# The second MLP projection, product by product over the whole inner layer

## The chip, the cores and the metric

The kernel runs on one core of a Trainium2 chip. The metric is the device time of one execution in microseconds (us); lower is better. TensorE does the matmuls, VectorE, ScalarE and GpSimd the elementwise work, and SyncE only issues DMAs, one after the other, between HBM and the on-chip memory.

## The reference

One layer: a token mixer (pooling and gated DeltaNet) with its two projections, then a squared-ReLU MLP, then a last RMSNorm. The change concerns the MLP and the last norm. S = 1024 tokens, D_MODEL = 1024, D_FF = 4096, float32.

```
def reference(x, norm_mix, w_in, ..., norm_mlp, w_up, w_down, norm_final):
    h = x
    ...                                   # token mixer
    h = h + mix @ w_out[l]
    u = rms_norm(h, norm_mlp[l])
    h = h + jnp.square(jax.nn.relu(u @ w_up[l])) @ w_down[l]
    return rms_norm(h, norm_final)
```

## The kernel before, in words

Precision: each float32 operand is split into a rounded half ("hi", a cast on ScalarE) and the rest ("lo", a subtraction on VectorE). A product is three matmuls, hi x hi, hi x lo and lo x hi (`mm3`, line 44 in the profile). In names, `wh`/`wl` are hi and lo of a weight tile, `th`/`tl` and `sh`/`sl` those of other operands.

Both MLP projections use Strassen's scheme in Winograd's form: matrices are cut into 2 x 2 quadrants, and 7 products of quadrants, with sums of quadrants as operands, take the place of 8. Products are numbered 1 to 7.

First projection (`up_ready`, `up_product`): the 4096 columns of the inner layer are taken in 16 pairs of 2 x 128. Per pair, a weight tile `wu` (1 MB) is loaded, GpSimd makes four sums of weight blocks, and each product is split and multiplied, 12 matmuls of 128x128 by 128x512. The tokens' operands TH[i], TL[i] of all seven products are made once, at `turn_second`, in the stretch called "the turn" below; products 1 and 2 of pairs 0 and 1 run ahead of it. Results are combined in `p1`, `u2`, `u3` (VectorE adds a bank; product 1 is copied by ScalarE) and become four quadrants of the hidden matrix after relu and square on ScalarE (`hidden`, lines 953 and 954): h11, h21 (in p1's tile), h12 (in u2's), h22 (in u3's). Each is written to HBM, into `hd[b]`, where b counts blocks of four pairs.

Second projection (`block_load`, `down_ready`, `sums`, `down_product`): for each of 4 blocks, eight 1 MB tiles are loaded, a11 to a22 of the hidden matrix and b11 to b22 of the weights. A step (b, i, s) is one product i on half s of the block: a split of its two operands (two casts and two subtractions of 128x1024), and 24 matmuls, six into each of four banks. Between steps, GpSimd (line 1053) turns the loaded tiles in place into the sums that later products need. After a product's second half, VectorE adds its four banks to the residual `ht` (line 1093). In the last block, products 3, 7 and 4 are followed by `final`: the last norm of a token tile, out of place in a tile `o`, with products of `o` and the norm's weight partly on GpSimd.

```
TARGET = {1: (0, 0), 6: (0, 1), 7: (1, 1), 4: (1, 0), 2: (0, 0), 5: (1, 1), 3: (0, 1)}
todo = [(b, i, s) for b in range(NB) for i in (1, 2, 5, 6, 3, 7, 4) for s in range(2)]
```

The order on each engine: TensorE's is the order of the code; the other engines' instructions are placed by a scheduler, which the diff does not show. Tiles come from pools with a number of buffers (`bufs`); a new tile in a full pool waits until the oldest one's readers are done. A tile of a pool that was opened in the room of a closed one waits for the readers of what lay there.

Of the kernel before, what the change touches and what calls it, by code (L numbers as in the profile page):

```python
# [28 lines left out]
def hybrid_trunk(ctx, tc, x, norm_mix, w_in, conv_w, w_pool, pool_scale, a_log, dt_bias,  # L29
# [203 lines left out]
    u_r = const.tile([P, P], F32R, name="u_r")  # L233
# [16 lines left out]
    for l in range(7):  # L250
        b = 1 << l
        m = const.tile([P, P], F16, name=f"lev{l}")
# [142 lines left out]
    def pool_group(i, acc, g, dst):  # L395
# [17 lines left out]
        if i == 0:  # L413
            hd = const.tile([P, 16], F32, name="hd", tag="gr")
# [479 lines left out]
    NPAIR, BQ = FF // 256, 4  # L894
    NB = NPAIR // BQ

    hd = [hdp.tile([P, 4, BQ, HALF], F32, name=f"hd{b}") for b in range(NB)]
    H11, H12, H21, H22 = range(4)
    wuv = w_up2.rearrange("(k p) f -> p k f", p=P)

    def turn_second(ys):

        for k in range(KT):
# [3 lines left out]
            A.activation(R[12 if k < 4 else 22][:, j, :], pt, AF.Copy, scale=nmlp[:, k:k + 1])  # L907
            if k < 4:
                V.tensor_tensor(R[11][:, j, :], R[12][:, j, :], R[11][:, j, :], op=ALU.subtract)
            else:  # L910
                V.tensor_tensor(R[2][:, j, :], R[22][:, j, :], R[11][:, j, :], op=ALU.subtract)
                G.tensor_tensor(R[12][:, j, :], R[22][:, j, :], R[12][:, j, :], op=ALU.subtract)
                G.tensor_tensor(R[21][:, j, :], R[21][:, j, :], R[2][:, j, :], op=ALU.subtract)
        for i, r in ((6, 2), (7, 12), (5, 11), (4, 21), (3, 22)):
# [3 lines left out]
            for j in range(4):  # L918
                A.copy(TH[i][:, j, :], R[r][:, j, :])  # L919
                V.tensor_tensor(TL[i][:, j, :], R[r][:, j, :], TH[i][:, j, :].bitcast(F32), op=ALU.subtract)  # L920
# [31 lines left out]
    def hidden(p, c, src, dst):  # L952
        A.activation(dst, src, AF.Relu)
        A.activation(dst, dst, AF.Square)
        nc.sync.dma_start(out=hd[p // BQ][:, c, p % BQ, :], in_=dst)

    def up_product(p, i, w):
# [7 lines left out]
        if i == 1:  # L965
            m["p1"] = cp.tile([P, HALF], F32, name="p1", tag="c")
            A.copy(m["p1"], acc)
        elif i == 2:
            hidden(p, H11, acc, cp.tile([P, HALF], F32, name="h11", tag="c"))
# [3 lines left out]
        elif i == 7:  # L973
            m["u3"] = ws.tile([P, HALF], F32, name="u3", tag="raw", bufs=3)
            V.tensor_tensor(m["u3"], acc, m["p1"], op=ALU.add)
        elif i == 5:
            V.tensor_tensor(m["u3"], acc, m["u3"], op=ALU.add)
            hidden(p, H22, m["u3"], m["u3"])
        elif i == 4:
            V.tensor_tensor(m["p1"], acc, m["p1"], op=ALU.add)  # L980
            hidden(p, H21, m["p1"], m["p1"])
# [180 lines left out]
```

## Time and profile before

| | us |
|---|---|
| median of 3 runs | 1203.25 (1201.89 to 1204.58) |
| profiled execution, its own time | 1201.03 |
| its span, first to last instruction | 1199.3 |
| TensorE busy | 1109.2 (92% of the span) |
| VectorE busy | 834.1 (70%) |
| ScalarE busy | 603.1 (50%) |
| GpSimd busy | 538.5 (45%) |
| mean granted TensorE clock | 0.987 |

| stretch of the span | us | what runs |
|---|---|---|
| 0 to 514 | 514 | token mixer and its projections |
| 514 to 570 | 56 | the turn, with products 1 and 2 of pairs 0 and 1 |
| 570 to 853 | 283 | first MLP projection |
| 853 to 1191 | 338 | second MLP projection |
| 1191 to 1199.3 | 8.3 | the last tiles' norm and their stores |

How to read the rows that follow. A row of groups or of one tile's instructions has the line, the engine, the operation, output <- input and the shapes, the count after x, then busy us and mean ns of one, and after the second bar the idle time of the engine just before them and what ended most of it. A row of the timeline is: start, duration, instruction, and in brackets the idle time before it with what ended it. A row of the windows has, for each engine, the busy time and the number of instructions in that stretch, the granted TensorE clock (1 is full), the mean busy share of the DMA engines, and GB/s. A row of the chain of waits is: start, length, the engine and line that the end of the program was waiting for. A DMA row ends with the KB of one and the median us from issue to landing.

### The profile page before, as it was taken

How to read it: one execution, taken by the hardware profiler on the slowest of the kernel's cores; microseconds unless marked ns; L12 is line 12 of the kernel's file. 1: busy time of each engine (PE TensorE's matmuls, PEld its weight loads, DVE VectorE, ACT ScalarE, POOL GpSimd, SP SyncE). 2: the span in 40 equal slices, each digit the busy share in tenths (PEclk: the TensorE clock that was granted, in tenths of full speed). 3: DMA queues.
4: the chain of work that ended last, by engine and by line, in shares of the span. 5: the costliest groups of instructions: out<-in, count | busy, mean ns of one | idle time of the engine just before them, and what ended most of it. 6: DMA issues, size and time to landing. Idle time of an engine off the chain costs nothing.

```text
span 1199.3 us, 15369 instructions
## 1 busy us (share of the span) xinstructions
PE 1109.2 (92%) x5606; PEld 890.2 (74%) x5606; DVE 834.1 (70%) x1206; ACT 603.1 (50%) x1119; POOL 538.5 (45%) x360
## 2 busy tenths in 40 slices
PE   6989998988898999967999999999988999999987
PEld 5777886767777788755788888888776777777865
DVE  6797598778788765678334343433589797888776
ACT  6657566665555463654545454545432333333435
POOL 6034355476563421063213232222298393575674
PEclk9999999999999999989999999999999999999999
DMA  5232211112123220211333323232855216011003
GB/s 165 81 113 89 71 50 48 45 45 54 54 62 119 89 79 28 80 62 46 112 110 111 118 94 123 97 114 97 316 193 175 71 35 213 34 35 70 1 1 141
DMA packets 69238, 109.08 MB, mean 91 GB/s; under 512 B 5477, under 2 KB 43434, under 8 KB 67114
## 3 DMA queue, kind: packets, MB, share of 16 engines
q1 hardware_dynamic: 69162, 108.09, 26.9%
q8 instruction: 44, 0.72, 0.2%
q14 instruction: 32, 0.26, 0.1%
HBM read 87.10 MB, written 20.97 MB: 90 GB/s over the span
## 4 chain that ended last, share of the span: by engine, by line
PE 55%; DVE 21%; issue 5%; POOL 4%; ACT 3%; DMA 1%; POOLq 0%; DVEq 0%; SPq 0%; ACTq 0%
PE bank L44 41%; PE acc L44 13%; DVE tl L926 5%; DVE sl L926 3%; DVE h L1093 2%; DVE cy L391 2%; POOL b L1053 2%; DVE tl L920 1%; DVE nxt L410 1%; ACT sh L925 1%; DVE xx L592 1%; POOL o L1109 1%; DMA a<-hd 1%; PE bank L48 1%; DVE nxt L409 0%
## 5 line engine op out<-in xcount | busy, mean ns | idle before, releaser
L44 PE MATMUL bank<-th,wh 128*128 128x512 f32 x448 | 178.5, 398 | 10.9 <-ACT th L919 7.4
L44 PE MATMUL bank<-tl,wh 128*128 128x512 f32 x448 | 178.3, 398 | 4.4 <-DVE tl L920 4.3
L44 PE MATMUL bank<-th,wl 128*128 128x512 f32 x448 | 177.5, 396 | 2.2 <-DVE wl L926 2.2
L925 ACT CAST sh<-a 128x1024 fp32r<-128x1024 f32 x54 | 56.7, 1050 | 198.8 <-PE bank L44 144.3
L1053 POOL TENSOR_TENSOR a<-a,a 128x1024 f32<-128x1024 f32 x32 | 97.4, 3053 | 107.2 <-DMA a<-hd 47.9
L44 PE MATMUL bank<-tl,sh 128*128 128x512 f32 x336 | 133.1, 396 | 11.8 <-DVE tl L926 11.6
L44 PE MATMUL bank<-th,sh 128*128 128x512 f32 x336 | 131.7, 392 | 2.4 <-ACT th L925 2.4
L926 DVE TENSOR_TENSOR wl<-wu,wh 128x512 fp32r<-128x512 f32 x112 | 80.1, 719 | 74.2 <-ACT wh L925 74.0
L44 PE MATMUL acc<-uh,wh 128*128 128x512 f32 x320 | 130.4, 408 | 1.2 <-DVE ul L173 0.7
L44 PE MATMUL bank<-th,sl 128*128 128x512 f32 x336 | 131.5, 392 | 0.0
L44 PE MATMUL acc<-ul,wh 128*128 128x512 f32 x320 | 129.3, 404 | 0.0
L925 ACT CAST wh<-wu 128x512 fp32r<-128x512 f32 x112 | 69.0, 620 | 118.9 <-PE bank L44 109.5
L44 PE MATMUL acc<-uh,wl 128*128 128x512 f32 x320 | 128.8, 402 | 0.0
L926 DVE TENSOR_TENSOR tl<-b,th 128x1024 fp32r<-128x1024 f32 x54 | 121.1, 2243 | 4.8 <-ACT th L925 4.8
L926 DVE TENSOR_TENSOR sl<-a,sh 128x1024 fp32r<-128x1024 f32 x54 | 89.2, 1651 | 41.1 <-ACT sh L925 41.1
L44 PEld LDWEIGHTS bank<-th,wh 128*128 128x128 f32 x448 | 85.0, 190 | 32.0 <-ACT th L919 8.1
L1053 POOL TENSOR_TENSOR b<-b,b 128x1024 f32<-128x1024 f32 x32 | 101.0, 3175 | 11.9 <-DVE tl L926 6.3
L44 PEld LDWEIGHTS bank<-tl,wh 128*128 128x128 f32 x448 | 84.8, 189 | 26.1 <-DVE tl L920 6.7
L44 PEld LDWEIGHTS bank<-th,wl 128*128 128x128 f32 x448 | 84.8, 189 | 23.1 <-DVE wl L926 3.1
L588 POOL TENSOR_TENSOR bl<-m,lev 128x512 f16<-128x512 f16 x48 | 62.1, 1293 | 82.6 <-PE bank L44 70.6
L942 POOL TENSOR_TENSOR wu<-wu 128x512 f32<-128x512 f32 x16 | 21.0, 1312 | 166.1 <-DVE wl L926 166.1
L44 PEld LDWEIGHTS bank<-tl,sh 128*128 128x128 f32 x336 | 63.5, 189 | 31.1 <-DVE tl L926 18.2
(318 smaller groups left out, 2494.2 us busy)
## 6 DMA issues: line engine op xcount, KB each, us to landing
raw<-in_w_in_dram SPq DMA_DIRECT2D x80, 256.0 KB, 2.7
wu<-in_w_up_dram SPq DMA_DIRECT2D x16, 1024.0 KB, 5.4
a<-hd SPq DMA_DIRECT2D x16, 1024.0 KB, 5.1
b<-in_w_down_dram SPq DMA_DIRECT2D x16, 1024.0 KB, 7.1
hd<-u SPq DMA_DIRECT2D x32, 256.0 KB, 2.0
raw<-in_w_out_dram SPq DMA_DIRECT2D x24, 256.0 KB, 2.7
xin<-in_x_dram SPq DMA_DIRECT2D x8, 512.0 KB, 4.9
h<-in_x_dram SPq DMA_DIRECT2D x8, 512.0 KB, 4.4
```

The costliest lines, as they stand in the source:

```text
L44: T0.matmul(out, lhsT, rhs, start=start, stop=stop, skip_group_check=goes_on)
L48: T0.transpose(out, in_, identity)
L391: V.scalar_tensor_tensor(cy, cr[:, e:e + HALF], tap[e], cy, op0=ALU.mult, op1=ALU.add)
L410: V.tensor_tensor(nxt[:, n:], cur[:, n:], cur[:, :W - n], op=ALU.add)
L588: G.tensor_tensor(bl, m1, bc(lev[l]), op=ALU.mult)
L592: V.tensor_tensor(xx, px, bc(ident), op=ALU.add)
L920: V.tensor_tensor(TL[i][:, j, :], R[r][:, j, :], TH[i][:, j, :].bitcast(F32), op=ALU.subtract)
L925: A.copy(hi, src)
L926: V.tensor_tensor(lo, src, hi.bitcast(F32), op=ALU.subtract)
L942: G.tensor_tensor(a11, a21, a11, op=ALU.subtract)
L1053: G.tensor_tensor(r[o], r[x], r[y], op=getattr(ALU, op))
L1093: V.tensor_tensor(hsl, acc, hsl, op=ALU.add)
```

## The change

The blocks go away. The second projection runs one product after the other, each over the whole inner layer: a step (i, s) is product i on pairs 2s and 2s+1, s = 0 to 7, with the products in the order 1, 2, 5, 6, 7, 3, 4.

- All seven left operands are kept in HBM. `hd[s][i]` is one 512 KB tile for each product and each two pairs. `keep` writes into it: h11, h21, h22 as before, and in place of h12 the four that `combine` makes on VectorE at the end of a pair: s1 = h12 + h22, s2 = s1 - h11, h11 - h12 (in u2's tile) and s4 = h21 - s2. These are 4 sums of 128x512 and 7 writes a pair in place of 4.
- `down_load` loads, for each step, one `x` tile (512 KB) and one or two `w` tiles (512 KB each; two for products 5 and 7): 56 and 72 loads. Four buffers each for x, the first w and the second w (`xr`, `wr`, `wr2`).
- The weight sums of products 5, 6, 7 and 4 are made by VectorE in `down_ready` (32 of 128x1024; `kept` holds those that later products use).
- The operands' splits have three buffers in place of two. Banks are added to the residual once per product, 28 times in place of 112.
- The last two steps of product 4 are multiplied together, so that each of its four banks ends with 12 matmuls of its own.
- `final` works in place in `ht`; its products with the norm's weight are all on VectorE, and the squares go to a `junk` tile.
- Ahead of it, many small constant tiles move from the pool `const` to the pool `gp`, which is closed before the MLP; R[22], h11, p1 and the new sums come from the pool `cp` with 9 buffers in place of 2; pair 1's u3 comes from there as well.

The diff, cut to what bears on the MLP:

```diff
-    u3 = lambda nm, dt: u3p.tile(ub, dt, name=nm, tag="u3", bufs=7)
-    R[12], R[22], R[2] = (u3(f"r{n}", F32) for n in (12, 22, 2))
-    cpc, cp = opened(name="cp", bufs=2, reuse_waits="tile")
+    u3 = lambda nm, dt: u3p.tile(ub, dt, name=nm, tag="u3", bufs=6)
+    R[12], R[2] = (u3(f"r{n}", F32) for n in (12, 2))
+    cpc, cp = opened(name="cp", bufs=9, reuse_waits="tile")
...
-    hd = [hdp.tile([P, 4, BQ, HALF], F32, name=f"hd{b}") for b in range(NB)]
+    hd = [{i: hdp.tile([P, 2, HALF], F32, name=f"hd{s}_{i}") for i in range(1, 8)} for s in range(NS)]
...
-    def hidden(p, c, src, dst):
+    def keep(p, i, t):
+        nc.sync.dma_start(out=hd[p // 2][i][:, p % 2, :], in_=t)
+
+    def hidden(src, dst):
         A.activation(dst, src, AF.Relu)
         A.activation(dst, dst, AF.Square)
-        nc.sync.dma_start(out=hd[p // BQ][:, c, p % BQ, :], in_=dst)
+
+    def combine(p):
+        m = tmp.pop(p)
+        h11, h21, h22, h12 = m["h11"], m["p1"], m["u3"], m["u2"]
+        s1, s2, s4 = c_tile("s1"), c_tile("s2"), c_tile("s4")
+        V.tensor_tensor(s1, h12, h22, op=ALU.add)
+        keep(p, 5, s1)
+        V.tensor_tensor(s2, s1, h11, op=ALU.subtract)
+        keep(p, 6, s2)
+        V.tensor_tensor(h12, h11, h12, op=ALU.subtract)
+        keep(p, 7, h12)
+        V.tensor_tensor(s4, h21, s2, op=ALU.subtract)
+        keep(p, 3, s4)
...
         elif i == 7:
-            m["u3"] = ws.tile([P, HALF], F32, name="u3", tag="raw", bufs=3)
+            m["u3"] = c_tile("u3") if p == 1 else ws.tile([P, HALF], F32, name="u3", tag="raw", bufs=3)
...
         else:
             V.tensor_tensor(m["u2"], acc, m["u2"], op=ALU.add)
-            hidden(p, H12, m["u2"], m["u2"])
+            hidden(m["u2"], m["u2"])
+            combine(p)
...
-    SUMS = {2: [("a21", "a21", "a22", "add"), ("b12", "b12", "b11", "subtract")],
-            5: [("a11", "a21", "a11", "subtract"), ("b12", "b22", "b12", "subtract")],
-            6: [("a12", "a12", "a11", "subtract")],
-            3: [("a11", "a22", "a11", "subtract"), ("b11", "b12", "b11", "subtract")],
-            7: [("b21", "b21", "b12", "subtract")]}
+    LOADS = {1: (11,), 2: (21,), 6: (22,), 5: (12, 11), 7: (22, 12), 3: (22,), 4: (21,)}
+    def down_load(i, s):
+        w = raw_w[(i, s)] = []
+        for n, blk in enumerate(LOADS[i]):
+            t = (wr if n == 0 else w2).tile(pair2, F32, name="w", tag="w")
+            e, c = blk // 10 - 1, blk % 10 - 1
+            nc.sync.dma_start(out=t, in_=wdv[s][e][:, :, c * HALF:(c + 1) * HALF])
+            w.append(t)
+        x = raw_x[(i, s)] = xr.tile(pair2, F32, name="x", tag="x")
+        nc.sync.dma_start(out=x, in_=hd[s][i])
+    def down_ready(i, s):
+        x, w = raw_x.pop((i, s)), raw_w.pop((i, s))
+        t = w[0]
+        if i == 5:
...
+            V.tensor_tensor(t, w[0], w[1], op=ALU.subtract)
...
+        (sh, sl), (th, tl) = (split(o, pair2, sp, f"{m}h", f"{m}l", 3) for o, m in ((x, "s"), (t, "t")))
...
+            A.activation(junk, ht[t][:, sl], AF.Square, scale=1.0 / 32, accum_out=st[:, n:n + 1])
+            V.tensor_tensor(ht[t][:, sl], ht[t][:, sl], nfin[:, sl], op=ALU.mult)
...
-    todo = [(b, i, s) for b in range(NB) for i in (1, 2, 5, 6, 3, 7, 4) for s in range(2)]
+    todo = [(i, s) for i in (1, 2, 5, 6, 7, 3, 4) for s in range(NS)]
+    for n, (i, s) in enumerate(todo):
+        while n_loaded < min(n + 4, len(todo)):
+            down_load(*todo[n_loaded])
+            n_loaded += 1
...
+        while n_made < min(n + 3, len(todo)):
+            ready[todo[n_made]] = down_ready(*todo[n_made])
+            n_made += 1
...
+        if (i, s) == (4, NS - 2):
+            continue
+        sets = [ready.pop((i, s))]
+        if (i, s) == (4, NS - 1):
+            sets.insert(0, ready.pop((i, s - 1)))
+        for t in range(4):
+            down_sums(i, t, sets, s == 0, s == NS - 1)
```

**Three places in the order of the instructions.** First SyncE's queue where the first projection ends and the second begins (the "seam"). Before, the writes of pair 15 stand between loads of the first block (line 955 is `hidden`'s write, line 1048 a block's load); these are the rows from the write of pair 15's h22 on:

```order
L955 DMA hd3_5794<-u3_8142 128x512
L1048 DMA b21_8217<-in_w_down_dram 128x4x512
L1048 DMA a21_8219<-hd0_5791 128x2048
L1048 DMA a22_8221<-hd0_5791 128x2048
L955 DMA hd3_5794<-p1_8084 128x512
L1048 DMA b12_8223<-in_w_down_dram 128x4x512
```

After (line 960 is `keep`, lines 1069 and 1072 the loads of w and x in `down_load`), again from the write of pair 15's h22 on:

```order
L960 DMA hd7_4_5842<-u3_8347 128x512
L960 DMA hd7_2_5840<-p1_8289 128x512
L1069 DMA w_8431<-in_w_down_dram 128x2x512
L1072 DMA x_8433<-hd0_1_5790 128x1024
L1069 DMA w_8435<-in_w_down_dram 128x2x512
L1072 DMA x_8437<-hd1_1_5797 128x1024
```

Before, three loads (a11, b11 and a12) stood still further ahead in this queue, among the writes of pairs 14 and 15; after, the first load of the second projection stands behind the write of pair 15's h21.

Second, VectorE at the end of a pair in the first projection. Before (lines 972 to 983 are the additions of a bank in `up_product`, line 926 the lo half of a split):

```order
L926 TENSOR_TENSOR wl_6803<-wu_6594,wh_6802 128x512
L983 TENSOR_TENSOR u2_6676<-bank_6720,u2_6676 128x512
L926 TENSOR_TENSOR wl_6822<-wu_6594,wh_6821 128x512
L926 TENSOR_TENSOR wl_6842<-wu_6594,wh_6841 128x512
L972 TENSOR_TENSOR u2_6819<-bank_6806,p1_6799 128x512
```

After (lines 971 to 977 are `combine`, line 933 the split, lines 997 and 1010 the additions):

```order
L933 TENSOR_TENSOR wl_6612<-wu_6383,wh_6611 128x512
L1010 TENSOR_TENSOR u2_6475<-bank_6519,u2_6475 128x512
L933 TENSOR_TENSOR wl_6631<-wu_6383,wh_6630 128x512
L971 TENSOR_TENSOR s1_6579<-u2_6475,u3_6513 128x512
L973 TENSOR_TENSOR s2_6580<-s1_6579,h11_6493 128x512
L975 TENSOR_TENSOR u2_6475<-h11_6493,u2_6475 128x512
L933 TENSOR_TENSOR wl_6651<-wu_6383,wh_6650 128x512
L977 TENSOR_TENSOR s4_6581<-p1_6455,s2_6580 128x512
L997 TENSOR_TENSOR u2_6628<-bank_6615,p1_6608 128x512
```

The four sums of `combine` stand between the last addition of one pair and the first of the next, among the next pair's splits.

Third, VectorE in the second projection. Before, around the end of product 6 in a block (line 926 the splits, line 1093 the additions to the residual; the sums are on GpSimd and do not show):

```order
L926 TENSOR_TENSOR sl_8493<-a11_8211,sh_8492 128x1024
L926 TENSOR_TENSOR tl_8497<-b12_8223,th_8496 128x1024
L926 TENSOR_TENSOR sl_8526<-a12_8215,sh_8525 128x1024
L1093 TENSOR_TENSOR h_4597<-bank_8259,h_4597 128x512
L926 TENSOR_TENSOR tl_8530<-b22_8225,th_8529 128x1024
L1093 TENSOR_TENSOR h_4597<-bank_8260,h_4597 128x512
```

After, in product 7 (line 1086 is its weight sum):

```order
L933 TENSOR_TENSOR sl_9700<-x_9653,sh_9699 128x1024
L933 TENSOR_TENSOR tl_9704<-w_9649,th_9703 128x1024
L1086 TENSOR_TENSOR w_9770<-w_9770,w_9772 128x1024
L933 TENSOR_TENSOR sl_9739<-x_9696,sh_9738 128x1024
L1086 TENSOR_TENSOR w_9809<-w_9809,w_9811 128x1024
L933 TENSOR_TENSOR tl_9743<-w_9692,th_9742 128x1024
L933 TENSOR_TENSOR sl_9778<-x_9735,sh_9777 128x1024
```

A sum of the weights now stands among the splits of each step of products 5, 6, 7 and 4, one or two steps ahead of the split that reads it, and the additions to the residual are gone from all steps but a product's last.

More of the change, by code (lines that the diff above doesn't have):

```diff
@@ L251, in hybrid_trunk @@
         b = 1 << l
-        m = const.tile([P, P], F16, name=f"lev{l}")
+        m = gp.tile([P, P], F16, name=f"lev{l}")
         nb = P // (2 * b)
@@ L320, in small @@
         def small(nm, dt=F32, keep=False):
-            return const.tile(sm, dt, name=f"{nm}{i}" if keep else nm, tag=f"{nm}{i}" if keep else nm)
+            return gp.tile(sm, dt, name=f"{nm}{i}" if keep else nm, tag=f"{nm}{i}" if keep else nm)
         pa = work_bank()
@@ L965, in up_product @@
         if i == 1:
-            m["p1"] = cp.tile([P, HALF], F32, name="p1", tag="c")
+            m["p1"] = c_tile("p1")
             A.copy(m["p1"], acc)
         elif i == 2:
-            hidden(p, H11, acc, cp.tile([P, HALF], F32, name="h11", tag="c"))
+            m["h11"] = c_tile("h11")
+            hidden(acc, m["h11"])
+            keep(p, 1, m["h11"])
         elif i == 6:
@@ L1050, in sums @@
-    def sums(b, s, what):
-        r = {k: v[:, 2 * s:2 * s + 2, :] for k, v in blocks[b].items()}
-        for o, x, y, op in what:
-            G.tensor_tensor(r[o], r[x], r[y], op=getattr(ALU, op))
-    SUMS = {2: [("a21", "a21", "a22", "add"), ("b12", "b12", "b11", "subtract")],
-            5: [("a11", "a21", "a11", "subtract"), ("b12", "b22", "b12", "subtract")],
-            6: [("a12", "a12", "a11", "subtract")],
-            3: [("a11", "a22", "a11", "subtract"), ("b11", "b12", "b11", "subtract")],
-            7: [("b21", "b21", "b12", "subtract")]}
@@ L1060, in hybrid_trunk @@
-    OPS = {1: ("a11", "b11"), 2: ("a12", "b21"), 3: ("a12", "b22"), 4: ("a22", "b21"), 5: ("a21", "b12"),
-           6: ("a11", "b12"), 7: ("a11", "b11")}
-    def down_ready(b, i, s):
-        r = blocks[b]
-        ops = [r[nm][:, 2 * s:2 * s + 2, :] for nm in OPS[i]]
-        if b == 0 and i == 1:
-            parts = [[split(o[:, q, :], [P, HALF], ws, "wh", "wl", 5) for o in ops] for q in range(2)]
-            out = [(*parts[q][0], *parts[q][1]) for q in range(2)]
-        else:
-            (sh, sl), (th, tl) = (split(o, [P, 2, HALF], sp, f"{m}h", f"{m}l", 2) for o, m in zip(ops, "st"))
-            out = [(sh[:, q, :], sl[:, q, :], th[:, q, :], tl[:, q, :]) for q in range(2)]
-        sums(b, s, SUMS.get(i, ()))
-        return out
+    wrc, wr = opened(name="wr", bufs=4, side="right", reuse_waits="tile")
@@ new lines, in hybrid_trunk @@
+    xrc, xr = opened(name="xr", bufs=4, side="right", reuse_waits="tile")
+    nfc, nf = opened(name="nf", bufs=1, side="right", reuse_waits="tile")
+    spc, sp = opened(name="sp", bufs=3, side="right", reuse_waits="tile")
+    w2c, w2 = opened(name="wr2", bufs=4, reuse_waits="tile")
+    pair2 = [P, 2, HALF]
+    nfin = nf.tile([P, D], F32, name="nfin")
+    wdv = w_down2.rearrange("(s q e p) n -> s e p q n", s=NS, q=2, e=2)
+    LOADS = {1: (11,), 2: (21,), 6: (22,), 5: (12, 11), 7: (22, 12), 3: (22,), 4: (21,)}
@@ L1097, in hybrid_trunk, with down_sums @@
-    outs = {}
-    def final(t, ns, last):
-        if t not in outs:
-            o = abp.tile([P, 2, D], F32, name="o", tag="ab") if t % 2 == 0 else outs[t - 1][0]
-            st = nf.tile([P, 2], F32, name="stf", tag="stf", bufs=8)
-            outs[t] = o, st
-        o, st = outs[t][0][:, t % 2, :], outs[t][1]
+    def down_sums(i, t, sets, first, last):
+        acc = chains[("a" if i in (1, 6, 7, 4) else "b", t)]
+        ts = slice(t * P, (t + 1) * P)
+        units = [u for ops in sets for u in ops]
+        for n, (sh, sl, th, tl) in enumerate(units):
+            mm3(acc, sh[:, ts], sl[:, ts], th, tl, first and i in (1, 2, 5) and n == 0, last and n == len(units) - 1,
+                i not in (1, 2, 5))
+        if last:
+            m, n = TARGET[i]
+            hsl = ht[CH * m + t][:, n * HALF:(n + 1) * HALF]
+            V.tensor_tensor(hsl, acc, hsl, op=ALU.add)
+            if i in (3, 7, 4):
+                final(CH * m + t, [0, 1] if i == 3 else [1] if i == 7 else [0], i != 7)
```

149 lines of the change are left out of this document (65 added, 84 removed).

## The prediction

> **What bounds the kernel now.** The windows come first, since the diff leaves everything ahead of the MLP alone: one stretch for the first MLP projection and one for the second.
>
> ```profile
> core 0: us, PE busy (x) PEld busy (x) DVE busy (x) ACT busy (x) POOL busy (x), PEclk, DMA share, GB/s
> 853.00:1191.00 338.00, 315.69 (x1346) 250.89 (x1344) 280.82 (x241) 123.89 (x149) 218.38 (x77) 0.99 0.27 100
> 570.00:853.00 283.00, 282.94 (x1212) 228.86 (x1213) 114.28 (x173) 141.80 (x236) 68.49 (x53) 0.99 0.32 113
> ```
>
> In the first projection TensorE is never idle and VectorE is at 40%. In the second VectorE is at 83%, GpSimd at 65%, and TensorE has gaps. The chain that ended last gives the edges and shows who fills it:
>
> ```profile
> 699.80 153.50 PE bank L44 x661
> ...
> 884.56 3.42 DVE sl L926
> 887.97 0.60 DVE h L1093
> 888.58 2.74 DVE tl L926
> ```
>
> So the second projection starts at 699.80 + 153.50 = 853.3. It ends with this matmul, at 1190.9:
>
> ```profile
> 1179.62 0.39 PE L44 MATMUL bank<-th,sl 128*128 128x512 f32 x1
> ...
> 1190.50 0.39 PE L44 MATMUL bank<-th,sl 128*128 128x512 f32 x1
> ```
>
> These rows are 48 matmuls apart: 10.88 / 48 = 0.227 us from start to start where nothing holds TensorE. The stage has 4 blocks x 7 products x 2 halves x 24 = 1344 matmuls, or 305.1 us at that pace, and it takes 337.6: 32.5 us are waits. The groups and one line's instructions say why VectorE is late:
>
> ```profile
> L926 DVE TENSOR_TENSOR tl<-b,th 128x1024 fp32r<-128x1024 f32 x54 | 121.1, 2243 | 4.8 <-ACT th L925 4.8
> L1053 POOL TENSOR_TENSOR b<-b,b 128x1024 f32<-128x1024 f32 x32 | 101.0, 3175 | 11.9 <-DVE tl L926 6.3 <-DVE h L1093 5.4
> L1053 POOL TENSOR_TENSOR a<-a,a 128x1024 f32<-128x1024 f32 x32 | 97.4, 3053 | 107.2 <-DMA a<-hd 47.9 <-issue 32.9 <-DVE sl L926 26.4
> L926 DVE TENSOR_TENSOR sl<-a,sh x54: 1207/1226/3444, 853.8 to 1181.0; 128x1024 fp32r<-128x1024 f32 x54
> L926 DVE TENSOR_TENSOR tl<-b,th x54: 1209/2816/3457, 857.3 to 1182.2; 128x1024 fp32r<-128x1024 f32 x54
> ```
>
> The same subtraction takes 1.21 us at best and up to 3.46. Which of the two it is goes with GpSimd, in the windows:
>
> ```profile
> 870.00:880.00 10.00, 9.80 (x44) 7.79 (x43) 6.93 (x7) 4.01 (x4) 10.00 (x4) 1.00 1.03 405
> 890.00:900.00 10.00, 8.12 (x34) 6.03 (x33) 10.00 (x7) 3.99 (x4) 10.00 (x4) 1.00 0.01 2
> 930.00:940.00 10.00, 10.00 (x46) 8.29 (x45) 6.33 (x6) 4.00 (x4) 1.92 (x1) 1.00 0.59 209
> ```
>
> With GpSimd busy throughout (890 to 900), VectorE is full and TensorE makes 34 matmuls; with GpSimd nearly idle (930 to 940), VectorE has room and TensorE makes 46. GpSimd's 64 sums are what the gaps come from, by slowing VectorE's splits.
>
> **The second projection, costed.** The matmuls stay 7 x 8 x 24 = 1344, so 305.1 us stay. GpSimd's 64 sums go. VectorE gets 32 sums of 128x1024 instead; no row has this sum on VectorE, and the nearest is the split's subtraction of the same size, 1.21 us undisturbed (upper end: 3.46 beside GpSimd, whose work is gone, so I take the lower). Evictions fall from 112 to 28:
>
> ```profile
> L1093 DVE TENSOR_TENSOR h<-bank,h 128x512 f32<-128x512 f32 x87 | 56.7, 680 | 11.6 <-PE bank L44 11.6
> ```
>
> VectorE's load is then 112 x 1.21 + 32 x 1.21 + 28 x 0.68 = 193 us of 305, and at worst 3.63 us (two splits, one sum) in a step of 24 matmuls, 5.45 us. Three split buffers instead of two let it run more than a step ahead. So I take the whole 32.5 us of waits as gone; what comes back is costed next.
>
> **What is late next: the loads at the seam.** SyncE issues in order. Before, most of the first block's loads were issued ahead of the last writes; now the first load stands behind the write of h21 of pair 15 (line 960 of the changed code, from p1), and the second weight tile also waits for the last matmul of the first projection, whose operand lay there.
>
> ```profile
> 851.26 0.63 ACT L953 ACTIVATE p<-p 128x512 f32<-128x512 f32 x1 [0.33 <-DVE p L980]
> xin<-in_x_dram SPq DMA_DIRECT2D x8, 512.0 KB, 4.9
> h<-in_x_dram SPq DMA_DIRECT2D x8, 512.0 KB, 4.4
> b<-in_w_down_dram SPq DMA_DIRECT2D x16, 1024.0 KB, 7.1
> raw<-in_w_out_dram SPq DMA_DIRECT2D x24, 256.0 KB, 2.7
> ```
>
> Relu starts 2.0 us before the seam and the square follows, so the write is issued about 0.5 us before it, and the first weight and x loads by 0.3 us after (0.3 to 0.4 us each to issue). A 512 KB load lands 4.4 us on: 4.7. Four casts at 0.62 and four subtractions at 0.68, in pairs, bring the last operand at 8.0. By then 6 of the product's 24 matmuls are done; 18 x 0.227 = 4.1 follow. And the clock drops after such a pause:
>
> ```profile
> 536.33 0.80 PE L44 MATMUL bank<-th,wh 128*128 128x512 f32 x1 [4.23 <-ACT th L919]
> 540.71 0.80 PE L44 MATMUL bank<-tl,wh 128*128 128x512 f32 x1 [3.58 <-DVE tl L920]
> ...
> 544.40 0.40 PE L44 MATMUL bank<-th,wl 128*128 128x512 f32 x1
> ```
>
> There eight matmuls took 3.69 us for 1.59, so 2.0 more. The seam costs 8.0 + 4.1 + 2.0 - 5.45 = 8.6 us; 6.9 with the 2.7 us of a 256 KB load, 11.3 with the 7.1 of a 1 MB load. The Trainium skill ("TensorE: Matmul & The Clock Gate", Part 1) says that the clock halves after an idle window of about 3.4 us and returns after about as long of sustained work: by it, 1.7 us in place of 2.0, and none if the loads land early enough to keep the pause under one window. The trace agrees in the first (pauses of 4.2 and 3.6 us, then half pace).
>
> Steady loads: 56 of x and 72 of w, 0.524 MB each, 67 MB where 100 GB/s x 338 us = 34 MB moved before. A step asks 1.05 MB (192 GB/s), in products 5 and 7 1.57 MB (289 GB/s). The 870 to 880 row moved 405 GB/s with TensorE at full pace, so they are covered; without that cover see the rivals. The Trainium skill ("DMA: Bandwidth & Descriptors", Measured) speaks against the change: batch transfers to 1 MiB or more to reach 75% of peak, and these go from 1 MB to 512 KB. Three quarters of 405 would be 304 GB/s, an estimate by that page; the sum would stand, with 5% to spare in products 5 and 7. No run so far shows 512 KB loads streaming.
>
> At the end, four banks of product 3 and their final norms come on top of splits: 4 x 0.68, 8 multiplications moved from GpSimd's share and 4 scalings, some 10 us of VectorE over four steps that have 4 x (5.45 - 3.63) = 7.3 to spare plus a step's lead: 0 to 4, I take 1.5. In the tail the last four tiles come 12 matmuls apart instead of 6, so VectorE has no queue (its last eviction starts 0.35 us after the last matmul, row below), but the multiplication by the norm's weight is now in place and waits for ScalarE's square (+0.68): +0.3.
>
> ```profile
> 1191.24 0.68 DVE L1093 TENSOR_TENSOR h<-bank,h 128x512 f32<-128x512 f32 x1
> ```
>
> **The first projection.** VectorE gets four 128x512 sums per pair, at the split's price:
>
> ```profile
> L926 DVE TENSOR_TENSOR wl<-wu,wh 128x512 fp32r<-128x512 f32 x96 | 65.9, 686 | 70.1 <-ACT wh L925 70.1
> 532.20 6.78 DVE L911 TENSOR_TENSOR r<-r,r 128x512 f32<-128x512 f32 x4
> 602.83 0.58 ACT L967 COPY p<-bank 128x512 f32<-128x512 f32 x1
> 622.33 0.58 ACT L967 COPY p<-bank 128x512 f32<-128x512 f32 x1
> ```
>
> A pair takes 19.5 us; VectorE's share goes from 12 x 0.69 = 8.3 to 11.0 us. Splits run up to five weight buffers ahead, so the burst hides. Writes go from 4 to 7 a pair (1.8 MB plus the 1 MB load in 19.5 us: 147 GB/s). Cost 0; next late would be the write of h11-h12, whose buffer is wanted again about 3 us after it has landed.
>
> Around the turn three things move. Pair 1's u3 has a buffer of its own, so this wait goes:
>
> ```profile
> 569.23 0.69 DVE L975 TENSOR_TENSOR u<-bank,p 128x512 f32<-128x512 f32 x1 [1.31 <-DMA hd<-u]
> 570.06 0.47 PE L44 MATMUL bank<-th,wh 128*128 128x512 f32 x1 [3.47 <-DVE u L975]
> 582.83 0.62 ACT L925 CAST wh<-wu 128x512 fp32r<-128x512 f32 x1 [0.55 <-PE bank L44]
> 583.36 0.58 ACT L967 COPY p<-bank 128x512 f32<-128x512 f32 x1
> 570.00:580.00 10.00, 9.94 (x36) 7.98 (x37) 3.28 (x5) 6.82 (x12) 2.58 (x2) 0.83 0.29 113
> ```
>
> That is 3.5 us, and 17% of 10 us at the lower clock: -5.2. The two h11 (0.58 + 0.62 us on ScalarE) now stand among the copies that feed VectorE there: +1.2. In pair 2 the copy of P1 stands behind a cast that waits for the product just ahead, and TensorE waits for it: 0.1 + 0.62 + 0.58 = +1.3. Together -2.7 (bounds -5.2 and 0).
>
> **The sum**, against the profiled execution: -32.5 + 8.6 + 1.5 + 0.3 - 2.7 = -24.8. Its time is 1201.0 (span 1199.3 and 1.7 around it), giving 1176.2; the median of the runs is 2.2 above it, so 1178.5.
>
> **The rivals.** (1) The seam is cheaper and the end free: the loads land in 2.7 us and no pause stays long enough for the slow clock: 8.6 becomes 4.9 and 1.5 becomes 0, so 1173. For it: 405 GB/s with several loads under way; against: a 512 KB row never landed below 4.4 in the median. (2) Products 5 and 7 starve. If 512 KB loads stream at 245 GB/s, 16 steps take 6.4 us instead of 5.45: +15, 1194; at 289 it starts. For it: 1 MB took 7.1 us, alone 148 GB/s; against: 405 GB/s. (3) VectorE becomes the first projection's limit: if every sum meets GpSimd and takes 1.7 us (as the four of line 911 did, 6.8 us) and the lead doesn't cover 1.5 us of it a pair, 16 x 1.5 = +24, no change, 1202. Against it: 15 of 19.5 us even so. (4) On the other side: the loads are served one after another. 128 x 4.4 us = 563 against 305: +258, near 1437. It decides from (305.1 + 24.8) / 128 = 2.6 us a load; 0.524 MB at 405 GB/s is 1.3. Slower only if a load takes twice that.
>
> **How the numbers follow.** The forecast 0.62 (1173 to 1185, from the seam's bounds and the turn's), (1) 0.12, (2) 0.13, (3) 0.04, (4) 0.05, and 0.04 for a wait not seen here that eats all of it, half of it above. Faster takes the first three and half of (3): 0.89; same the rest of (3) and half of the last: 0.04; slower 0.07. A difference under 0.2% (2.4 us) can't be told from none in this kernel, whose three runs span 2.7 us. The range leaves out (3), (4), the unseen and a part of (2): 1169 to 1194.
>
> **What would show it.** In the profile after: GpSimd nearly idle in the second projection; sl and tl at 1.21 to 1.25 us; TensorE at 44 to 46 matmuls in 10 us from 20 us past the seam on; one gap of 5 to 7 us at the seam and a clock below 1 after it; no gap near 566; DMA at 190 to 290 GB/s. Wrong would be: casts that wait for x or w loads in products 5 and 7, VectorE above 80% there, or gaps once a pair in the first projection.

## The result, and the profile after

The changed kernel takes 1173.49 us (median of 4 runs, 1171.99 to 1176.83) and the kernel before 1203.69 (median of 4, 1201.89 to 1204.58): a ratio of 0.9755, 95% interval 0.9731 to 0.9779. Forecast were 1178.5 and a range of 1169 to 1194. The profiled executions, 1201.03 and 1173.46, with spans of 1199.3 and 1171.7, are 27.6 us apart, and the stages below add up to that.

| stage, us | before | after | difference | forecast |
|---|---|---|---|---|
| up to the first matmul of the first projection | 513.94 | 513.58 | -0.4 | 0 |
| from there to its last matmul (the turn and the pairs) | 338.95 | 336.76 | -2.2 | -2.7 |
| from there to the last matmul of the second projection | 337.61 | 313.69 | -23.9 | -22.4 |
| behind it | 8.8 | 7.7 | -1.1 | +0.3 |

All are taken from start to start of TensorE's rows. "The second projection" below is the third of these stages, 337.6 and 313.7 us.

The windows of the changed kernel over the second and the first projection, then over one stretch of 10 us in product 1 and one around the change from product 2 to 5:

```profile
850.00:1164.00 314.00, 307.76 (x1347) 253.76 (x1346) 201.14 (x206) 127.29 (x152) 6.83 (x6) 0.99 0.66 229
567.00:850.00 283.00, 282.04 (x1222) 229.25 (x1221) 150.97 (x232) 140.31 (x233) 71.74 (x55) 1.00 0.42 146
870.00:880.00 10.00, 10.00 (x46) 8.26 (x45) 4.81 (x4) 4.11 (x4) 0.00 (x0) 1.00 1.04 395
940.00:950.00 10.00, 10.00 (x45) 8.28 (x45) 9.50 (x11) 4.00 (x4) 0.00 (x0) 1.00 1.05 391
```

GpSimd has gone from 218 us to 6.8, VectorE from 281 to 201, and TensorE is short of the full 314 by 6.2 us only, the pause at the seam. In the steady stretches it makes 45 or 46 matmuls in 10 us, also where VectorE is nearly full (940 to 950) and while 391 to 395 GB/s are loaded. The splits, by line, with minimum, median and maximum in ns:

```profile
L933 DVE TENSOR_TENSOR sl<-x,sh x55: 1208/1225/1226, 860.1 to 1149.0; 128x1024 fp32r<-128x1024 f32 x55
L933 DVE TENSOR_TENSOR tl<-w,th x39: 1209/1218/1226, 858.9 to 1150.1; 128x1024 fp32r<-128x1024 f32 x39
```

No split takes more than 1.23 us, where the maximum before was 3.46. The seam, in the timeline: what SyncE issues, the first operand, and TensorE's first matmuls.

```profile
850.02 0.32 SPq L960 DMA_DIRECT2D hd<-p  x1
850.43 0.39 SPq L1069 DMA_DIRECT2D w<-in_w_down_dram  x1
850.87 0.49 SPq L1072 DMA_DIRECT2D x<-hd  x1
...
855.76 0.62 ACT L932 CAST wh<-x 128x512 fp32r<-128x512 f32 x1 [2.98 <-DMA x<-hd]
...
856.95 0.79 PE L44 MATMUL bank<-wh 128*128 128x512 f32 x1 [6.22 <-ACT wh L932]
...
861.77 0.40 PE L44 MATMUL bank<-wl,wh 128*128 128x512 f32 x1
```

The write of h21 is issued 0.3 us before the last matmul of the first projection starts (850.34), the loads stand behind it, and the cast begins when x lands, 4.9 us after its issue. TensorE pauses for 6.22 us and then makes its first ten matmuls in 4.8 us, 0.43 us or more apart instead of 0.227.

### The profile page after: what moved, and what is told of

Its sections match the earlier page's. It is cut to its first block, busy times and chain, and to the rows that moved or that the text cites. A ratio compares the mean times of both kernels' runs of the same rounds, so it can differ in the third digit from the quotient of the medians.

```text
span 1171.7 us, 15587 instructions
## 1 busy us (share of the span) xinstructions
PE 1099.8 (94%) x5606; PEld 893.7 (76%) x5606; DVE 786.6 (67%) x1224; ACT 602.8 (51%) x1117; POOL 327.1 (28%) x288
## 4 chain that ended last, share of the span: by engine, by line
PE 71%; DVE 12%; ACT 3%; issue 2%; POOL 2%; DMA 0%; POOLq 0%; DVEq 0%; ACTq 0%; SPq 0%
PE bank L44 53%; PE acc L44 17%; DVE cy L391 2%; DVE tl L927 1%; DVE nxt L410 1%; DVE xx L592 1%; PE bank L48 1%; DVE nxt L409 0%; DMA x<-hd 0%; DVE r L918 0%; ACT th L172 0%; DVE ul L173 0%; DVE ml L764 0%; DVE m L546 0%; DVE kn L533 0%
## 5 line engine op out<-in xcount | busy, mean ns | idle before, releaser
L932 ACT CAST sh<-x 128x1024 fp32r<-128x1024 f32 x55 | 57.9, 1054 | 160.9 <-PE bank L44 154.2
L933 DVE TENSOR_TENSOR sl<-x,sh 128x1024 fp32r<-128x1024 f32 x55 | 67.3, 1223 | 88.1 <-ACT sh L932 88.0
L152 POOL TENSOR_TENSOR stf<-stf,mhalf 128x1 f32<-128x1 f32 x8 | 7.9, 998 | 329.7 <-DVE stf L1125 329.7
L391 DVE SCALAR_TENSOR_TENSOR cy<-cr,cols,cy 128x512 f32<-128x512 f32 x72 | 74.1, 1034 | 8.2 <-ACT cy L389 7.7
L133 POOL TENSOR_TENSOR wl<-raw,wh 128x512 fp32r<-128x512 f32 x48 | 68.0, 1421 | 36.4 <-ACT wh L132 36.2
L44 PEld LDWEIGHTS bank<-th,sl 128*128 128x128 f32 x344 | 64.6, 188 | 13.5
L44 PEld LDWEIGHTS bank<-th,sh 128*128 128x128 f32 x344 | 64.6, 188 | 13.5
```

Of the source, the lines that this page charges most:

```text
L44: T0.matmul(out, lhsT, rhs, start=start, stop=stop, skip_group_check=goes_on)
L133: eng.tensor_tensor(lo, raw, hi.bitcast(F32), op=ALU.subtract)
L152: last["rsqrt"] = G.tensor_tensor(s, s, mhalf[:, :n], op=ALU.pow)
L391: V.scalar_tensor_tensor(cy, cr[:, e:e + HALF], tap[e], cy, op0=ALU.mult, op1=ALU.add)
L932: A.copy(hi, src)
L933: V.tensor_tensor(lo, src, hi.bitcast(F32), op=ALU.subtract)
```

## The experiments

Each kernel is the kernel before or the changed one with a single edit, or with two or three of these edits together. Times are medians; ratios are to the kernel before, run on the same chip beside it; the second projection is measured in the profiled execution as above.

| kernel | us | ratio (95%) | second projection, us |
|---|---|---|---|
| before | 1203.69 | 1 | 337.6 |
| changed | 1173.49 | 0.9755 (0.9731 to 0.9779) | 313.7 |
| before, sums on VectorE | 1194.29 | 0.9931 (0.991 to 0.9953) | 324.6 |
| changed, a GpSimd sum per step | 1183.44 | 0.984 (0.9806 to 0.9873) | 324.3 |
| changed, 84 additions more | 1175.29 | 0.9765 (0.9729 to 0.98) | 315.7 |
| changed, short lead | 1177.03 | 0.9781 (0.975 to 0.9811) | 318.0 |
| changed, GpSimd sums and short lead | 1201.78 | 0.9972 (0.995 to 0.9994) | 343.1 |
| changed, all three | 1233.37 | 1.024 (1.0201 to 1.0279) | 374.9 |
| changed, weight sums on GpSimd | 1175.62 | 0.9764 (0.9726 to 0.9803) | 316.0 |
| the same with the short lead | 1188.12 | 0.9889 (0.9861 to 0.9917) | 326.8 |
| changed, first loads ahead | 1163.46 | 0.9681 (0.9663 to 0.9699) | 304.7 |
| changed, weight loads doubled | 1176.23 | 0.9778 (0.9752 to 0.9803) | 313.8 |
| changed, h11 behind the turn | 1173.20 | 0.9758 (0.9736 to 0.9779) | 313.9 |
| before, u3 apart | 1198.63 | 0.9973 (0.9955 to 0.9992) | 339.4 |

The last column comes from one execution of each kernel. Three kernels whose second projection should cost the same have 313.7, 313.8 and 313.9 us; one more stretch of 3.4 us at half clock adds up to 1.7 us (last row).

### GpSimd's sums alone, from both sides

Before, with its 64 sums on VectorE:

```diff
-            G.tensor_tensor(r[o], r[x], r[y], op=getattr(ALU, op))
+            V.tensor_tensor(r[o], r[x], r[y], op=getattr(ALU, op))
```

> The kernel before with one part of the change: GpSimd's 64 sums of the second projection go to VectorE, all else (112 evictions, two split buffers, block order, 1 MB loads) as before. Theory (GpSimd slows VectorE's splits): splits at 1.21 to 1.25 us, VectorE 112 x 1.21 + 64 x 1.21 + 112 x 0.68 = 289 us, the second projection falls from 337.6 to 306-320 us, the time to 1170-1186. Rival (what made VectorE late is its own work and the short lead, which the new order halves): VectorE at 289 of 305 with sums queued ahead of splits, the second projection stays at 328 or more, the time at 1193 or more.

The second projection took 324.6 us: 13.0 of the 32.5 us of waits went, neither theory's number. The splits, by line, show that the contention itself was gone almost throughout:

```profile
L926 DVE TENSOR_TENSOR sl<-a,sh x54: 1207/1224/1739, 861.2 to 1175.5; 128x1024 fp32r<-128x1024 f32 x54
L926 DVE TENSOR_TENSOR tl<-b,th x54: 1208/1215/1226, 864.7 to 1176.6; 128x1024 fp32r<-128x1024 f32 x54
```

So 19.5 us of waits are left with splits at full speed. The run isn't clean, though: it puts the 64 sums into VectorE's queue. The longest wait of TensorE, 3.29 us at 904.82, is for the last of these splits, whose cast was done at 897.67:

```profile
895.54 2.35 DVE L1053 TENSOR_TENSOR b<-b,b 128x1024 f32<-128x1024 f32 x2
897.81 0.68 DVE L1093 TENSOR_TENSOR h<-bank,h 128x512 f32<-128x512 f32 x1
898.41 1.21 DVE L1053 TENSOR_TENSOR a<-a,a 128x1024 f32<-128x1024 f32 x1
...
901.28 2.35 DVE L1053 TENSOR_TENSOR a<-a,a 128x1024 f32<-128x1024 f32 x2
903.55 1.21 DVE L926 TENSOR_TENSOR tl<-b,th 128x1024 fp32r<-128x1024 f32 x1
```

Sums and additions, none of them slowed, stand in a row ahead of a split that is made only one step ahead. That is the rival's mechanism, beside the theory's. (The median fell by 8.8 us. Up to the second projection this kernel's instructions stand in the same order as before; its profiled execution was 3.7 us later all the same at the start of the first projection and lost 3.8 in it, mostly at a lower clock, so that only the stage is compared.)

The changed kernel with a sum per step on GpSimd:

```diff
+        G.tensor_tensor(ghost, x, x, op=ALU.add)
```

> The changed kernel with 56 sums of 128x1024 on GpSimd, one per step, whose result nobody reads (about 174 us of GpSimd; the kernel before had 64). Theory (contention): splits beside GpSimd take up to 3.4 us, their mean goes from 1.22 to 1.6-2.2, VectorE's busy time in the second projection from 202 to 260-310 us, and where a sum of the weights comes on top (products 5, 6, 7, 4) TensorE waits again: +5 to +25 us. Rival (fewer evictions and the longer lead made the gain): within 2 us of the changed kernel, whatever the splits take.

```profile
L933 DVE TENSOR_TENSOR sl<-x,sh x55: 1206/1224/2914, 868.8 to 1162.7; 128x1024 fp32r<-128x1024 f32 x55
L933 DVE TENSOR_TENSOR tl<-w,th x39: 1209/2315/2917, 869.9 to 1163.9; 128x1024 fp32r<-128x1024 f32 x39
853.00:1178.00 325.00, 311.79 (x1348) 253.95 (x1346) 273.08 (x206) 126.63 (x152) 148.14 (x63) 0.98 0.66 222
```

The same 206 VectorE instructions now take 273 us in place of 201; sums on GpSimd do slow the splits. But TensorE lost 10.6 us only, and 5.7 of them in the first step, where nothing has been made ahead (its 24 matmuls took 13.8 us, 8.0 without the sums). The other 55 steps lost 4.9 us. With two steps of lead the slow splits are mostly absorbed. (The sums that nobody reads are lighter than those they stand for: one of 2.5 us a step, 141 us in all, where the kernel before had 64 of 3.1 us, 198 us, up to two a step.)

### Evictions and lead

```diff
+        if s % 2 and s < NS - 1:
+            for n in range(4):
+                V.tensor_tensor(ghost, x[:, n % 2, :], x[:, 1 - n % 2, :], op=ALU.add)
```

> The changed kernel with the 84 evictions back that went, as VectorE additions of 128x512 that nobody reads (84 x 0.68 = 57 us). Theory: VectorE goes from 202 to 259 of 314 us and hides it, 0 to +2 us. Rival (the evictions made VectorE late): +5 to +15 us.

315.7 us, 2.0 more, 0.6 of it at the seam: the evictions that went had been hidden but for about 1 us.

```diff
-    (name="sp", bufs=3) ... f"{m}l", 3) ... min(n + 3, len(todo))
+    (name="sp", bufs=2) ... f"{m}l", 2) ... min(n + 2, len(todo))
```

> The changed kernel with two split buffers in place of three and operands made one step ahead in place of two. Theory: two casts and two subtractions in series take 1.05 + 1.05 + 1.22 = 3.3 us after a buffer comes free, 5.45 are there: 0 to +2 us. Rival (the lead made the gain): TensorE waits at each weight sum, +8 us or more.

318.0 us, 4.3 more: above the theory's 2 and below the rival's 8. Neither accounts for 32 us alone, so they were put together.

> The changed kernel with the sum on GpSimd per step and the short lead, without the additions: VectorE has about 278 us. If the two add up, 10.6 + 4.3 = 15 us: 328.6 us in the second projection. Theory (a lead of one step can't level out splits of 1.2 and 3.4 us): 330 to 340. Rival (the lead doesn't matter where VectorE is the limit): 324 to 327.

343.1 us, 29.4 more, where the two alone had 10.6 and 4.3. Less what the seam has of it (3.2, in the first step), 26.2 against 4.9 + 4.3. TensorE's waits name the reason, the lo halves of the splits; columns are total us, times and the longest:

```profile
PE bank L44 <- DVE tl L933: 9.5, 10, 2.8
PE acc L44 <- DVE tl L933: 7.9, 9, 1.5
...
849.00:1192.00 343.00, 316.41 (x1345) 253.18 (x1344) 265.95 (x205) 127.00 (x153) 136.56 (x62) 0.98 0.63 209
```

VectorE is busy for 266 of 343 us, less than in the run with the long lead, and yet late nineteen times. So in the changed kernel it isn't VectorE's total that counts, but whether a step with slow splits can borrow time from the step before.

> The changed kernel with all three put back together: a sum on GpSimd per step that nobody reads, 84 additions on VectorE, two split buffers with one step of lead. Alone they lengthened the second projection from 313.7 us to 324.3, 315.7 and 318.0, so 17 us if they add up: 331. Theory (they meet in VectorE's queue, which has 278 us with the sums and 335 with the additions as well, more than the 305 of TensorE): 336 to 350 us, the whole gain back or more. Rival (the new order of products is worth something by itself): 325 to 333.

374.9 us, far beyond the theory's 350, with VectorE at 323 of 375 us. The queue was not full, so the theory's picture, a sum of busy times, was wrong and only its direction right. Part of the reason is the stand-in for the evictions:

```profile
L1082 DVE TENSOR_TENSOR ghost<-x 128x512 f32<-128x512 f32 x84 | 83.4, 993 | 16.9 <-DMA x<-hd 16.2
```

These additions read the tile x that is just being loaded. Before nine of them VectorE stood idle, 16.2 us in all, until x had landed, with splits behind them in its queue; an eviction reads a bank and the residual, and waits for no load. They also took 83 us in place of the 57 reckoned. So this run overstates the evictions, and how much of the 31.8 us beyond the run without them is an eviction's cost stays open. The sum per step and the additions with the long lead have no time: with three split buffers and the two extra tiles the kernel is too large for the on-chip memory.

### Where the sums of the weights are made

```diff
-            V.tensor_tensor(t, w[0], w[1], op=ALU.subtract)
+            G.tensor_tensor(t, w[0], w[1], op=ALU.subtract)
```

(and so for all four products)

> The changed kernel with its 32 sums of the weights on GpSimd in place of VectorE. Theory (contention): the sums take 2.5 to 3.1 us each there, the splits beside them 1.4 to 2.1 on average in products 5, 6, 7 and 4; VectorE gives up 39 us and gets some 25 to 45 back, and a sum in place now takes longer than the splits that wait for it: +2 to +10 us on the changed kernel. Rival (half as many sums and the longer lead make GpSimd harmless): within 2 us.

316.0 us, 2.3 more, at the lower end. That VectorE makes the sums of the weights is worth 2.3 us here. With the short lead as well:

> The changed kernel with its 32 sums of the weights on GpSimd and the short lead (two split buffers, operands one step ahead): what is left of the change is the new order with its left operands from HBM and the fewer additions. Alone these two lengthened the second projection from 313.7 us to 316.0 and 318.0, so 320.3 if they add up. Theory (the short lead is what lets the slow splits through to TensorE, as with the sums that nobody reads, where 10.6 and 4.3 us became 29.3): 324 to 336, and the waits in products 5, 6, 7 and 4. Rival (GpSimd is idle for long enough between its sums): 318 to 322.

326.8 us, 13.1 more (0.4 of it at the seam), where 2.3 and 4.3 would have made 6.6. Here too the two together cost about twice their sum. The waits stand in products 5 and 4, not in 6 and 7. At 326.8 us the second projection is still 10.8 us shorter than before. That part belongs to what this run keeps of the change: half as many sums, fewer evictions, the order of the products and the left operands from HBM. It was not taken apart further.

### The seam

```diff
+    def load_ahead(i, s):
+        bt = big_tile("ahead", [4, HALF])
+        nc.sync.dma_start(out=bt[:, 0:2, :], in_=wsrc)
+        nc.sync.dma_start(out=bt[:, 2:4, :], in_=hd[s][i])
...
+        if e == (NPAIR - 1, 1):
+            for a in AHEAD:
+                load_ahead(*a)
```

(`AHEAD` is steps (1, 0) and (1, 1); `down_load` takes these tiles for them)

> The changed kernel with the loads of its first two steps moved ahead of the last pairs' writes, into two tiles of the pool of big tiles, which are free by then. Theory (the seam's 8.6 us are the late first loads, the split behind them and the slow clock after the pause): the gap of 6.2 us and the half pace behind it go, the second projection falls from 313.7 to 305.5-308 us, 5.5 to 8.5 us faster than the changed kernel. Rival (the wait only moves to the third step's loads, which still start at the seam): 0 to 3 us faster, a gap of 4 us or more two steps later.

```profile
849.00:1154.00 305.00, 305.00 (x1347) 252.32 (x1345) 197.74 (x202) 124.06 (x149) 6.82 (x6) 1.00 0.66 228
850.00:860.00 10.00, 10.00 (x45) 8.22 (x44) 8.21 (x10) 5.39 (x7) 0.00 (x0) 1.00 0.94 342
```

TensorE is busy for all of the 305 us and at the full clock: 304.7 us for 1344 matmuls, 9.0 less than the changed kernel. Nothing took the place of the wait. At 1163.46 us (ratio 0.9681) this kernel beats both. The edit changes two things at once, the place in SyncE's queue and the tiles. The queue had a part in the wait: here the third step's loads go into the tiles that the changed kernel has for its first, and the first of them is issued at 846.42, ahead of the write of pair 15's h21 (850.25) and 2.7 us before the last matmul of the first projection starts. In the changed kernel, behind that write, the first load is issued 0.1 us after that start. So a tile was free earlier than the queue let a load begin; the place in the queue alone was not tried.

### The loads

```diff
-    LOADS = {1: (11,), 2: (21,), 6: (22,), 5: (12, 11), 7: (22, 12), 3: (22,), 4: (21,)}
+    LOADS = {1: (11, 12), 2: (21, 22), 6: (22, 21), 5: (12, 11), 7: (22, 12), 3: (22, 21), 4: (21, 22)}
```

> The changed kernel with a second weight tile loaded in every step, 40 loads of 512 KB more that nobody reads: 1.57 MB in a step of 5.45 us, 289 GB/s through all of the second projection. Theory (the loads are covered; the trace moved up to 399 GB/s): 0 to +3 us, and that at the seam alone. Rival (products 5 and 7 are covered only by what was loaded ahead of them, and 512 KB loads sustain 245 GB/s): 6.4 us a step, +20 to +40 us.

```profile
860.00:1140.00 280.00, 279.99 (x1224) 231.23 (x1225) 182.36 (x182) 115.11 (x134) 5.72 (x4) 0.99 0.89 317
880.00:890.00 10.00, 10.00 (x45) 8.28 (x45) 4.70 (x4) 2.91 (x3) 0.00 (x0) 1.00 1.04 396
```

317 GB/s over 280 us, and TensorE never idle: 313.8 us, no more than without. The 2.7 us in the median lie elsewhere (its profiled execution was 2.3 us late already at the first projection).

### The turn

```diff
-            m["u3"] = ws.tile([P, HALF], F32, name="u3", tag="raw", bufs=3)
+            m["u3"] = big_tile("u3", [4, HALF])[:, 0, :] if p == 1 else ws.tile([P, HALF], F32, name="u3", tag="raw", bufs=3)
```

> The kernel before with one part of the change: pair 1's u3 in a tile of its own, so that it doesn't wait for an earlier write. Theory: the wait of 3.47 us at 570 goes, and with it the slow clock behind it (1.7 us): 3.5 to 5.5 us faster than before. Rival (another operand is late at the same place): the wait stays at 2 us or more, under 2 us faster.

The wait at 570 was gone, and the stage from the turn to the last pair was 3.8 us shorter (335.18 against 338.95); the median fell by 3.3 us. (The second projection, where nothing was changed, took 1.8 us longer in this execution: behind two pauses at 1147 and 1149 the clock was halved for 6.8 us, and for 3.4 in the kernel before.) That the clock's share is not in the 3.8 us has to do with an earlier pause. The first rows are this kernel's behind the pause of 3.20 us, the others those of the kernel before at the same place:

```profile
553.46 0.76 PE L44 MATMUL bank<-th,wh 128*128 128x512 f32 x1 [3.20 <-ACT th L919]
554.02 0.63 PE L44 MATMUL bank<-tl,wh 128*128 128x512 f32 x1
...
556.58 0.49 PE L44 MATMUL bank<-tl,wh 128*128 128x512 f32 x1
```

```profile
552.48 0.47 PE L44 MATMUL bank<-th,wh 128*128 128x512 f32 x1 [3.20 <-ACT th L919]
552.79 0.40 PE L44 MATMUL bank<-tl,wh 128*128 128x512 f32 x1
```

The same pause was followed by seven matmuls at half pace here (some 1.4 us) and by none there.

```diff
+            if p < 2:
+                held.append((p, acc))
...
             turn_second(ys)
+            for p, acc in held:
+                hidden(acc, tmp[p]["h11"])
+                keep(p, 1, tmp[p]["h11"])
```

> The changed kernel with relu, square and write of the first two h11 put behind the turn again, as they ran before. Theory (these four instructions of 0.6 us among ScalarE's copies at the turn make the pauses there longer, 4.35 us in place of 3.20 at 552, and a pause that long halves the clock for what follows): the pause at 537 falls from 6.4 by 1 us or more, the one at 553 under 3.4 us, 2 to 3.5 us faster than the changed kernel. Rival (the turn waits for VectorE's subtractions anyway): within 1 us.

The rival was nearer: the pauses got shorter as the theory says, 6.38 to 5.21 and 4.35 to 3.12 us, but the stage by 0.5 us only. The clock was halved all the same:

```profile
552.33 0.77 PE L44 MATMUL bank<-th,wh 128*128 128x512 f32 x1 [3.12 <-ACT th L926]
552.89 0.63 PE L44 MATMUL bank<-tl,wh 128*128 128x512 f32 x1
```

## Why the prediction was right, and where it was not

**The waits of the second projection: the size right, the cause half right.** That all 32.5 us would go was right: with the seam out of the way, 304.7 us are left of the 305.1 that the pace gives. That "GpSimd's 64 sums are what the gaps come from, by slowing VectorE's splits" is borne out where the gaps of the kernel before stand close together, from 884.69 to 924.83:

```profile
884.70:924.80 40.10, 34.46 (x144) 26.54 (x144) 40.10 (x25) 11.95 (x13) 39.00 (x12) 1.00 0.30 101
```

These are six steps of 6.7 us in place of 5.45, in which VectorE has no idle time and GpSimd next to none. But it was not the whole cause. Taking the slow splits away alone gave 13.0 us of 32.5, with the sums' own time put into VectorE's queue. In the changed kernel slow splits with a lead of two steps cost 4.9 us outside the seam, a lead of one step with fast splits 4.3, both together 26.2: there the gaps come back only where slow splits meet a short lead, and the change removed both. The sentence "Three split buffers instead of two let it run more than a step ahead" stood in the prediction as a reason more; by these runs it carried as much as the other. What a longer lead alone would do for the kernel before is not shown. In the six steps above VectorE falls behind by 7.4 us (6 x 1.24), of which one more step of lead could cover 5.45, an estimate. The comparison of VectorE's 193 us (201 measured) with TensorE's 305 did not carry the argument: in the run of 343.1 us VectorE had 266 and was late all the same.

**The seam: right.** Forecast 8.6 us, measured 9.0 by taking it away. Of the parts, the pause came to 6.22 (forecast 5 to 7), x landed 4.9 us after its issue (taken 4.4), and the first step's 24 matmuls behind the pause took 2.6 us longer than at full pace (2.0 for the clock). The rows behind the 2.0 hold seven matmul intervals, not eight, and give 2.1.

**The end of product 3: too dear by 1.5.** No matmul waited there. The tail was forecast at +0.3 and came to -1.1: the wait for the square is there (0.62 us), but the queue that it replaces was longer than I saw. In the kernel before, the last tile's multiplication did not follow its addition of 1191.24, but stood behind work on other tiles:

```profile
1191.84 0.68 DVE L1109 TENSOR_TENSOR o<-h,nfin 128x512 f32<-128x512 f32 x1
1192.44 0.48 DVE L1113 TENSOR_SCALAR o<-o,stf 128x512 f32<-128x512 f32 x1
1192.84 0.15 DVE L1111 SCALAR_TENSOR_TENSOR stf<-stf 128x1 f32<-128x1 f32 x1
1193.13 0.69 DVE L1109 TENSOR_TENSOR o<-h,nfin 128x512 f32<-128x512 f32 x1
```

I had read VectorE's queue off the start of its last addition alone; it lay behind that. The last store is issued 4.1 us after the last matmul has ended now (1168.53 against 1164.42), and 4.8 before (1195.71 against 1190.89).

**The turn: -2.2 against -2.7, by parts that erred both ways.** The wait for u3's write went (3.47 us), as forecast, and pair 2 waits for its copy, 0.96 us where 1.3 were forecast:

```profile
584.49 0.50 PE L44 MATMUL bank<-th,wh 128*128 128x512 f32 x1 [0.96 <-ACT p L990]
```

The h11 of pairs 0 and 1 made the pause at 553 longer by 1.15 us (1.2 forecast), and behind it ten matmuls ran at half pace, some 2 us that I had not counted, because the kernel before had none there. That the clock would go with the length of a pause was my error. Up to 585 us the parts come to -0.8: some +3.3 ahead of the wait for u3, -5.2 for that wait and its slow clock, +1.0 for pair 2. The other -1.4 is spread over the pairs behind it, whose 1151 matmul intervals are 0.2310 us long on average instead of 0.2322. The prediction has no term for it, and its cause stays open; that the sum came near -2.7 is partly luck.

**The loads: right.** No starving in products 5 and 7 (rival 2), nor loads one by one (rival 4), at 317 GB/s sustained; the changed kernel's loads came to 229 GB/s over the projection, within the 190 to 290 forecast, and to 395 in stretches. The Trainium skill ("DMA: Bandwidth & Descriptors", Measured) has the rule to batch to 1 MiB or more. Going below it cost nothing here: loads of 512 KB ran at that rate, against the 405 GB/s of 1 MB loads before. **The first projection** hid `combine`, as forecast: beyond pair 2 TensorE has no wait in it.

## What to carry to other kernels

An engine that is 80% busy and makes the limiting engine wait can be relieved in two ways: make its instructions even, or give it more lead. In the changed kernel either alone kept all but 4 to 11 us of what the loss of both cost (29); so a part of a change that seems to do nothing may be what the rest leans on. Before a stage's first product, ask which load it waits for and what stands ahead of it in the queue: loads moved further ahead, into tiles that were free by then, were worth 9 us.

## What the runs showed of the hardware that was not expected

The clock behind a pause of TensorE is not set by the pause's length alone. At the same place of the turn a pause of 3.20 us was followed by full pace in one execution and by half pace in another, one of 3.12 us by fourteen slow matmuls, and one of 4.34 us by three matmuls at full pace and then eight slow ones:

```profile
552.59 0.47 PE L44 MATMUL bank<-th,wh 128*128 128x512 f32 x1 [4.34 <-ACT th L926]
552.90 0.40 PE L44 MATMUL bank<-tl,wh 128*128 128x512 f32 x1
553.13 0.46 PE L44 MATMUL bank<-th,wl 128*128 128x512 f32 x1
553.39 0.63 PE L44 MATMUL bank<-th,wh 128*128 128x512 f32 x1
```

The Trainium skill ("TensorE: Matmul & The Clock Gate", Part 1) says that the window of about 3.4 us in which activity is judged runs freely and is not reset when a kernel starts. The granted clock agrees with that; these are windows of the changed kernel:

```profile
544.40:551.10 6.70, 4.17 (x17) 2.76 (x16) 6.67 (x7) 0.62 (x1) 4.05 (x3) 1.00 0.00 0
551.20:557.90 6.70, 4.42 (x11) 3.49 (x12) 6.34 (x11) 2.70 (x5) 0.00 (x0) 0.50 0.01 2
558.00:854.90 296.90, 291.77 (x1263) 236.83 (x1261) 160.10 (x247) 146.49 (x243) 71.74 (x55) 1.00 0.41 144
```

In its trace the clock was halved from 534.09 to 544.33, from 551.15 to 557.98 and from 854.94 to 861.77 us: three, two and two steps of 3.413 us, which begin 5 and 94 such steps after the first. In all fourteen traces the clock changes on a grid of that step, placed differently in each. What the halving goes with is how long TensorE was idle within one step of the grid. Behind 530 us, all 43 steps at full clock with over 1.9 us of idle time were followed by half clock, and only one of 2502 with less (1.80 us). The pause of 3.20 us that cost nothing lay across two steps, 1.48 and 1.72 us; the one behind which the pace halved had 3.11 us in one. So a pause of about that length costs nothing or some 3 us, by where it falls on the grid, and a difference of 2 us between two executions around such a pause says nothing of the kernels.

GpSimd slowed VectorE where both operands are ordinary on-chip tiles (in SBUF), and not where one is a bank that TensorE writes. In the kernel before, the splits went to 3.46 us, but the additions of a bank to the residual stayed as they were, although about half of them ran wholly beside a GpSimd sum:

```profile
L1093 DVE TENSOR_TENSOR h<-bank,h x88: 673/678/693, 862.6 to 1191.2; 128x512 f32<-128x512 f32 x88
```

Additions of the same size with two ordinary tiles did not stay so, in the run with all three:

```profile
L1082 DVE TENSOR_TENSOR ghost<-x x84: 676/680/2380, 859.4 to 1196.2; 128x512 f32<-128x512 f32 x84
```

The Trainium skill ("GPSIMD Engine Reference", 1. Specifications) names two SBUF inputs as a condition of contention, and the trace agrees. So the 112 evictions before were never slowed, and the 84 additions that stood in for them beside GpSimd's sums were dearer than the evictions had been.
